# Two transformer blocks on one core: the second experts' order turned by sixteen, a hinted branch, and earlier weight splits in the first mixer

## The chip, the cores and the metric

The kernel runs on one core of a Trainium2 chip. The metric is the device time of one execution in microseconds (us), the median of several runs. TensorE (PE) does the matmuls, VectorE (DVE), ScalarE (ACT) and GpSimd (POOL) the elementwise work, and SyncE (SP) issues the loads of the weights.

## The reference, cut to what matters

Two different blocks follow each other on 256 tokens of width 1024, all in fp32. Each is a mixer (attention and a second branch, joined by an output projection) and a mixture of 32 experts in four groups of eight, of which a token uses two of one group. Cut to its core:

```python
# block 1: hybrid mixer, experts with 256 hidden columns, a shared expert
z = hp @ w_in                                   # c_q, c_kv, k_pe, gate_b, gate_c, x_in
q = rms_norm(c_q, q_norm) @ w_uq;  kv = rms_norm(c_kv, kv_norm) @ w_ukv
attn = causal_block_attention(...)              # 8 heads, 16 meta tokens ahead
conv = gate_b * sum(conv_w[k] * shifted(gate_c * x_in, k) for k in range(3))
h = h + rms_norm(concat(rms_norm(attn), rms_norm(conv)) @ w_out, post_mix_norm)
h = h + rms_norm(hier_moe(rms_norm(h, pre_ffn_norm)), post_ffn_norm)
# block 2: differential attention and retention, experts with 512 hidden columns
g_idx = argmax(softmax(t @ router_group + b));  e_idx = top_2(softmax(t @ router_expert + b)[g_idx])
routed = sum over the two experts of weight * (silu(t @ w_gate[e]) * (t @ w_up[e])) @ w_down[e]
```

The number of tokens that an expert gets depends on the data. With the inputs that the reference makes, every second-block expert has between 1 and 44 tokens but one: the thirtieth (index 29) has none. In the first block no expert has more than 32.

## The kernel before, in words

The program runs straight through: mixer 1, experts 1, mixer 2, experts 2, final norm. Weights stream through 26 slots of SBUF, each of 8 KB per partition. `plan()` is the fixed order of all weight chunks (1 MB each), and `Builder.load` issues them on SP's queue in that order. `ahead()` issues the next load whenever a slot has come free, so a load waits for the matmuls that last read its slot, and at most eight loads are under way.

**Experts 2** work in 16 units of two neighbouring experts, with room for 64 tokens per expert. A unit p has eight chunks of gate and up weights (`gu2`, even chunk numbers for the first expert of the unit, odd ones for the second) and four of down weights (`dn2`, likewise). The order is gu of unit p, then dn of unit p-1; only at the end dn of unit 14 comes ahead of gu of unit 15, with dn of unit 15 last. On PE a unit is `gate_up` (L1565, 64 matmuls), `down` of the unit before (L1645, 32 matmuls), a gather for every second unit (L1399), a transpose (L1592) and a scatter (L1671). Unit 15's down weights go through `quarters` (L1617). A load into a slot that held a chunk of these experts is conditional on the expert having tokens:

```python
e = 2 * key[1] + key[2] % 2          # some(), L276: expert of the chunk
return {"cond": self.loads_of[e] > 0}
```

The count is read into SP's registers. For an expert without tokens the transfer is left out, while its slot is still taken and the matmuls still run on what the slot held. An expert index 29 is the odd half of unit 14; index 13 would be the odd half of unit 6.

**Overflow.** `overflow()` (L1716) handles experts with more tokens than a unit holds (32 in block 1, 64 in block 2). It is a run-time branch, `tc.If` at L1738, built once for each block, after the fifth unit from the end is begun. With these inputs its body never runs.

**Mixer 1.** Many matmuls here multiply in three passes of a high and a low part. `prepare()` (L317) makes the parts of one half chunk: ACT copies 1024 columns to the high part (L329), and DVE (first half of a chunk) or POOL (second half) subtracts it for the low part (L330). `part()` hands the next prepared half to the matmuls (L354 to L356) and prepares another. `conv(i)` (L604) runs four such halves; `conv(0)` leaves its products in `u` (L622), later ones gate and filter (L631, L634). Ahead of `conv(0)` stands the norm of the compressed query and key, `cn` (L568 to L601, DVE, with a power on POOL at L366). `cn` is transposed into `cqT` (L657), which the query matmul (L675) reads. After the attention scores, `P` is normalised (L757 to L760, first half of the heads on DVE, second on POOL), transposed (L790), and `attend` (L805, L810) makes the output, whose projection is the last `w_out`, reading `ma`. At the end stands the first matmul of experts 1 (L1574).

Of the kernel before, what the change touches and what calls it, by code (L numbers as in the profile page):

```python
# [17 lines left out]
AF = mybir.ActivationFunctionType  # L18
OP = mybir.AluOpType
# [4 lines left out]
T = 256  # L24
# [51 lines left out]
def layout(i):  # L76
    f = {k: np.asarray(v) for k, v in i.items()}
    g = lambda n: f[n][0]
    o = {}
# [17 lines left out]
    def experts(n, wg, wu, wd):  # L97
        x, fw = 128 // CAP[n], wg.shape[2]
        fc = CH // (x * 512)
        if n == 2:  # L100
            gu = np.concatenate([wg, wu], 2).reshape(16, 2, 4, 2, 128, 1024).transpose(0, 2, 1, 4, 3, 5)
            dn = wd.reshape(16, 2, 4, 128, 2, 512).transpose(0, 4, 1, 3, 2, 5)
        else:
            gu = np.concatenate([wg, wu], 2).reshape(32 // x, x, 8, 128, 2 * fw).transpose(0, 2, 3, 1, 4)
            dn = wd.reshape(32 // x, x, fw // (128 * fc), fc, 128, 2, 512).transpose(0, 5, 2, 4, 3, 1, 6)
        o[f"gu{n}"], o[f"dn{n}"] = gu.reshape(-1, 8, 128, CH), dn.reshape(-1, 4, 128, CH)

    experts(1, g("w_gate"), g("w_up"), g("w_down"))
    experts(2, g("expert_w_gate_2"), g("expert_w_up_2"), g("expert_w_down_2"))
    last = g("expert_w_down_2")[30:].reshape(2, 4, 128, 4, 256).transpose(3, 2, 1, 0, 4)  # L110
    o["dn2"] = np.concatenate([o["dn2"][:-1], last.reshape(1, 4, 128, CH)], 0)
    w = kt(g("w_in_2"))
    nat = lambda a: w[:, :, a:a + 512].reshape(128, 2, CH).transpose(1, 0, 2)
    tr = lambda a: w[:, :, a:a + 512].reshape(128, 8, 2, 2, 128).transpose(2, 0, 3, 1, 4).reshape(2, 128, CH)
    o["wi2"] = np.stack([nat(1024), tr(0), tr(512), nat(2560), tr(1536), nat(2048)])
    o["wo2"] = kt(g("w_out_2")).reshape(128, 4, CH).transpose(1, 0, 2)
    o["wr"] = np.stack([np.concatenate([kt(g(a)), np.zeros((128, 8, 4), np.float32), kt(g(b))], 2).reshape(128, 320)
                        for a, b in (("w_group_router", "w_expert_router"),
                                     ("router_group_w_2", "router_expert_w_2"))])
    o["pmg"] = g("post_mix_norm")  # L120
    col = lambda v, n: v.reshape(n, 128).T
    row = lambda v: np.broadcast_to(v.reshape(1, -1), (128, v.size))
# [8 lines left out]
        "br2": np.concatenate([row(g("router_group_b_2")), pad, row(g("router_expert_b_2"))], 1),  # L131
# [59 lines left out]
class Builder:  # L191
# [120 lines left out]
    def bank(self):  # L312
        return self.ps.tile([128, 512], F32, name="bank")
# [126 lines left out]
    def mixer1(self):  # L440
# [86 lines left out]
                                   accum_out=ss[:, 3 * e + 1:3 * e + 2])  # L527
        V.tensor_tensor(ss[:, 0:3], ss[:, 0:3], ss[:, 3:6], op=OP.add)
        rx = self.rms(ss[:, 0:3], 3, D)
        ang = sub([128, 2, 3, 16])  # L530
        posf = sub([128, 3])
        nn = sub([128, 2, 3, 16])
# [20 lines left out]
        A.activation(sc, ang, AF.Sin)  # L553
        sin, cos = sc[:, 0], sc[:, 1]
        self.free(meta)
        self.prepare(2, V)
        nc.scalar.dma_start(cT[:, 1536:2048], self.a["c3"])
        rxx = sub([128, 258])

        def spread_rx():  # L560
            p = bank()
            self.spread(p[:, 0:NM], rx[:NM, 2:3], NM)
            for t in range(2):
                self.spread(p[:, NM + t * 128:NM + t * 128 + 128], rx[:, t:t + 1])
            A.activation(rxx, p[:, NM - 2:TA], AF.Square)

        ss2 = sub([128, 5])
        V.memset(ss2, 1.0)  # L568
# [23 lines left out]
        ru = sub([128, 256])  # L592
        rv = sub([128, 256])

        def rope(dst, src, cosb, sinb, n):
            u = ru[:, :32 * n].rearrange("p (a b c) -> p a b c", b=2, c=16)
            v = rv[:, :32 * n].rearrange("p (a b c) -> p a b c", b=2, c=16)
            V.tensor_tensor(u, src, cosb, op=OP.mult)
            V.tensor_tensor(v, src, sinb, op=OP.mult)
            V.tensor_tensor(dst[:, :, 0], u[:, :, 0], v[:, :, 1], op=OP.subtract)  # L600
            V.tensor_tensor(dst[:, :, 1], u[:, :, 1], v[:, :, 0], op=OP.add)  # L601
# [6 lines left out]
        def conv(i, done, then=(), between=()):  # L608
            for m in range(4):
                if m in then:  # L610
                    then[m]()
                w = self.part()
                c = w.rearrange("p s (k c) -> p s k c", k=8)
                p = bank()
                for k in range(8):
                    self.mm3(p[:, :258], (c[:, 0, k], c[:, 1, k]), (xh[k], xl[k]), k == 0, k == 7)
                if m in between:
                    between[m]()
                done(m, p[:, :258])
                self.free(w)  # L620

        conv(0, lambda m, p: V.tensor_tensor(u[:, m], p, rxx, op=OP.mult),  # L622
             between={0: spread_rx})

        vy = self.slot([128, 2048], "vy")
        v = vy[:, 0:1024].rearrange("p (t c) -> p t c", t=2)
# [14 lines left out]
        ckT = cT[:, 512:512 + TA]  # L641
        vm = cT[:, 1024:1536]
        pm = [(cT[:, 1536 + 256 * t:1664 + 256 * t], cT[:, 1664 + 256 * t:1792 + 256 * t]) for t in range(2)]
        pk = bank()
        PE.transpose(pk[:, 0:NM], cn[:NM, 2, 256:384], id_[:NM, :NM])
        for t in range(2):
# [5 lines left out]
        pq = bank()  # L652
        for j in range(2):
            for t in range(2):
                PE.transpose(pq[:, j * T + t * 128:j * T + t * 128 + 128], cn[:, t, j * 128:j * 128 + 128], id_)
        for j in range(2):
            V.tensor_scalar(cqT[:, j], pq[:, j * T:j * T + T], s["qn"][:, j:j + 1], None, op0=OP.mult)  # L657
# [98 lines left out]
        for e in range(2):  # L756
            for t in range(2):  # L757
                f = sm[:, t, 4 * e:4 * e + 4]
                V.reciprocal(f, f)
                (nc.gpsimd if e else V).tensor_tensor(P4(t, e), P4(t, e), f[:, :, None].to_broadcast(  # L760
                    [128, 4, 144 if t == 0 else TA]), op=OP.mult)
        self.free(gen)
        pT1 = self.slot([128, 2, 8, 128], "pT")
        at = cT[:, 0:1024].rearrange("p (t m q) -> p t m q", t=2, m=4)
# [54 lines left out]
                w_out(pc, mc, t, e, 2, w[0])  # L819
        for t in range(2):  # L820
            feat_tot(sq, t)
        self.prepare(2)
        self.phase(0, 6)
        turn_p(0, 0)
        turn_p(0, 1)
# [4 lines left out]
            w_out(pc, mc, 1, e, 3, w[1])  # L830
        turn_p(1, 1)
        self.free(*PP, *w, mc)
        rc = feat_rstd(rx[:, 0:2])
        turn_m(0)
        turn_m(1)
        mix = self.slot([128, 2, D], "mix")
        ma = self.slot([128, 2, 4, T], "ma", F32R)
        for t in range(2):
            for e in range(2):
                A.activation(mix[:, t, e * 512:e * 512 + 512], pc[t, e], AF.Copy, scale=rc[:, t:t + 1])  # L840
            attend(t)
        self.phase(0, 7)
        w = [self.part() for _ in range(4)]
        self.free(pT1, cT)
# [93 lines left out]
    def mixer2(self):  # L938
# [328 lines left out]
class MoE:  # L1267
# [215 lines left out]
    def run(self, after):  # L1483
# [236 lines left out]
        def overflow():  # L1720

            own = [b.slot([128, CH], "own") for _ in range(6)]
            b.quiet = True
            empty, b.empty = b.empty, collections.deque(b.held.pop(id(t))[0] for t in own if b.trace)
            ov = [b.slot([128, CH], "over") for _ in range(2)]
            keep = b.slot([128, 4, 512], "keep")
            xo = b.slot([128, 2, 8, 128], "xo")
            loads = [0]

            def load_over(name, *at):  # L1730
                t = ov[loads[0] % 2]
                loads[0] += 1
                nc.gpsimd.dma_start(t, a[name][at])
                return t

            over = nc.values_load(self.cnt[0:1, 0:1], min_val=0, max_val=T)
            held = 3 if n == 1 else 2
            with tc.If(over > C, preferred_fallthrough_block=False):  # L1738
                V.tensor_copy(keep[:, 3, :FW], hids[:, held, :FW])
                V.tensor_copy(keep[:, 2, 0:2], rs)  # L1740
                with tc.For_i(0, T // C - 1, 1):
                    V.tensor_scalar(rank, rank, float(-C), None, op0=OP.add)
                    slots(True)
# [77 lines left out]
```

## Time and profile before

| what | value |
|---|---|
| runs | 949.15, 949.41 and 949.89 us, median 949.41 |
| profiled execution | 944.73 us, of which the span from first to last instruction is 942.9 |
| PE busy | 853.1 us, 90% of the span |
| weight queue (q1) | 333.24 MB, its packets fill 86.5% of the span |
| mean granted TensorE clock | 0.946 of full speed |

Shares over the whole span hide the stages. Where the DMA share of a stretch stands at 1.01 the 16 DMA engines are full (about 420 GB/s), and where PE is busy for the whole of a stretch it waits for nothing. [...]

### The profile page before, as it was taken

Reading aid. Unit: us, or ns where it says so; the run is one execution under the profiler, and the core shown is the slowest. Engines: PE = TensorE matmul, PEld = TensorE weight load, DVE = VectorE, ACT = ScalarE, POOL = GpSimd, SP = SyncE. Lnnn points to the kernel's source line nnn. Section 1 sums busy time; section 2 is a strip of 40 time slices with the busy share of each in tenths; the row PEclk is TensorE's granted clock in tenths of the full one; section 3 lists DMA queues with packets and bytes.
Section 4 is the critical chain, followed back from the end, with each engine's and each line's share of the span. In section 5 each row is a group of like instructions: output and inputs, shape, how many; then the busy total and the mean of one; then the engine's idle time right before and its main releaser. Section 6 shows DMA issues by size and latency. Waiting matters only on the chain. (4 is left out here: it accounts for less than half of the span.)

```text
span 942.9 us, 12656 instructions
## 1 busy us (share of the span) xinstructions
PE 853.1 (90%) x4825; PEld 477.4 (51%) x4825; DVE 382.6 (41%) x787; ACT 228.3 (24%) x474; POOL 118.1 (13%) x83
## 2 busy tenths in 40 slices
PE   8899789999768777997999999999999998699995
PEld 6868565554313325897875444434343432334333
DVE  5766455244222248567552233233333312232233
ACT  5446332121101124653412112111111100111113
POOL 4321330000000038724310000000000000000002
PEclk8999989999878887997999999999999999899998
DMA  9927458999999999834688999999999999999981
GB/s 362 416 85 283 158 201 357 421 419 420 418 421 421 421 421 421 340 121 147 268 307 336 420 394 383 422 421 421 422 421 420 421 421 420 417 421 421 419 370 45
DMA packets 48187, 335.74 MB, mean 356 GB/s; under 512 B 5344, under 2 KB 5856, under 8 KB 8432
## 3 DMA queue, kind: packets, MB, share of 16 engines
q1 hardware_dynamic: 47072, 333.24, 86.5%
q10 hardware_dynamic: 1040, 1.54, 0.5%
q8 instruction: 43, 0.70, 0.3%
q14 instruction: 32, 0.26, 0.1%
HBM read 340.00 MB, written 1.05 MB: 362 GB/s over the span
## 5 line engine op out<-in xcount | busy, mean ns | idle before, releaser
L1565 PE MATMUL bank<-chunk,xe 128*64 128x512 f32 x1024 | 227.0, 599 | 8.6 <-issue 6.4
L1565 PEld LDWEIGHTS bank<-chunk,xe 128*64 128x64 f32 x1024 | 73.7, 138 | 152.7 <-issue 143.0
L1645 PE MATMUL bank<-chunk,hids 128*64 128x512 f32 x480 | 111.2, 594 | 4.5 <-DMA chunk<-in_dn_dram 4.5
L1574 PE MATMUL bank<-chunk,xe 128*32 128x512 f32 x512 | 66.1, 656 | 18.3 <-DMA chunk<-in_gu_dram 11.8
L330 POOL TENSOR_TENSOR w<-chunk,w 128x1024 fp32r<-128x1024 f32 x28 | 70.1, 2516 | 86.2 <-ACT w L329 73.4
L1660 DVE SCALAR_TENSOR_TENSOR ys<-bank,wc,ys 128x512 fp32r<-128x512 f32 x46 | 34.5, 750 | 101.8 <-ACT ys L1659 101.8
L1645 PEld LDWEIGHTS bank<-chunk,hids 128*64 128x64 f32 x480 | 35.4, 137 | 76.9 <-issue 66.0
L1580 DVE TENSOR_TENSOR hids<-bank,hids 128x512 f32<-128x512 f32 x12 | 8.3, 691 | 156.2 <-PE bank L1565 156.2
L1659 ACT ACTIVATE ys<-bank,wc 128x512 fp32r<-128x512 f32 x46 | 31.6, 687 | 142.6 <-PE bank L1645 107.7
L1243 POOL TENSOR_TENSOR out<-acc,rows 128x256 f32<-128x256 f32 x6 | 4.2, 730 | 437.7 <-DVE acc L1774 437.7
L329 ACT ACTIVATE w<-chunk 128x1024 fp32r<-128x1024 f32 x52 | 52.2, 1049 | 25.3 <-DVE w L330 11.5
L1678 DVE TENSOR_TENSOR acc<-acc,bank 128x512 f32<-128x512 f32 x84 | 52.1, 681 | 13.2 <-PE bank L1671 13.2
L1585 DVE SCALAR_TENSOR_TENSOR hids<-bank,misc,hids 128x256 f32<-128x256 f32 (+1 forms) x12 | 6.9, 573 | 114.2 <-ACT hids L1584 71.1
L1406 PEld LDWEIGHTS bank<-GS,h 128*128 128x128 f32 x384 | 46.6, 202 | 11.1 <-issue 5.4
L1671 PE MATMUL bank<-ys,GS 128*128 128x512 f32 x184 | 49.5, 408 | 1.4 <-ACT ys L1659 1.3
L1579 ACT ACTIVATE hids<-bank 128x512 f32<-128x512 f32 x12 | 7.2, 597 | 179.8 <-PE bank L1565 179.8
L1406 PE MATMUL bank<-GS,h 128*128 128x128 f32 x384 | 48.9, 288 | 1.6 <-DVE GS L1414 1.6
L1574 PEld LDWEIGHTS bank<-chunk,xe 128*32 128x32 f32 x512 | 15.8, 115 | 61.7 <-issue 59.7
L1656 PE MATMUL bank<-chunk,hids 128*32 128x512 f32 x256 | 36.1, 677 | 10.4 <-DMA chunk<-in_dn_dram 9.3
L330 DVE TENSOR_TENSOR w<-chunk,w 128x1024 fp32r<-128x1024 f32 x24 | 35.7, 1496 | 10.8 <-ACT w L329 10.8
L1584 ACT ACTIVATE hids<-bank,misc 128x256 f32<-128x256 f32 (+1 forms) x12 | 6.5, 545 | 136.3 <-PE bank L1574 88.4
L1006 PE MATMUL bank<-w,xT 128*128 128x512 f32 x144 | 37.7, 421 | 0.7 <-DVE xT L960 0.6
(409 smaller groups left out, 1260.3 us busy)
## 6 DMA issues: line engine op xcount, KB each, us to landing
chunk<-in_gu_dram SPq DMA_DIRECT2D x192, 1024.0 KB, 18.3
chunk<-in_dn_dram SPq DMA_DIRECT2D x95, 1024.0 KB, 19.8
chunk<-in_wi_dram SPq DMA_DIRECT2D x12, 1024.0 KB, 19.5
chunk<-in_wo_dram SPq DMA_DIRECT2D x8, 1024.0 KB, 15.4
chunk<-in_wc_dram SPq DMA_DIRECT2D x6, 1024.0 KB, 14.6
chunk<-in_sgu_dram SPq DMA_DIRECT2D x2, 1024.0 KB, 16.7
chunk<-in_wa_dram SPq DMA_DIRECT2D x4, 416.0 KB, 6.3
xt<-in_xt_dram SPq DMA_DIRECT2D x2, 512.0 KB, 4.3
```

Source lines behind the costliest of these rows:

```text
L329: self.nc.scalar.activation(w[:, 0], raw, AF.Copy)
L330: (eng or (self.nc.vector, self.nc.gpsimd)[e]).tensor_tensor(w[:, 1], raw, w[:, 0].bitcast(F32), op=OP.subtract)
L1006: PE.matmul(p[t], xT[x][:, 2 * i + k, t * 128:t * 128 + 128], w[:, s, k * 512:k * 512 + 512], start=i + x + s + k == 0, stop=i + x == 4 an ...
L1406: b.nc.tensor.matmul(self.pb[k // 4][:, k % 4 * 128:k % 4 * 128 + 128], b.h[:, t, k * 128:k * 128 + 128], G[:, t].bitcast(F32), start=t == ...
L1565: PE.matmul(g[i][e * C:e * C + C], xe[:, k + kk, e * C:e * C + C], cs[e][:, kk * 1024 + i * 512:kk * 1024 + i * 512 + 512], start=k + kk = ...
L1574: PE.matmul(g[i][e * C:e * C + C], xe[:, k, e * C:e * C + C], c[:, e, i * 512:i * 512 + 512], start=k == 0, stop=k == 7)
L1645: PE.matmul(y[e * C:e * C + C], hT[:, f * 128 + e * C:f * 128 + e * C + C], cs[e][:, f * 512:f * 512 + 512], start=f == 0, stop=f == 3)
L1656: PE.matmul(y[e * C:e * C + C], hT[:, o:o + C], c[:, f, e], start=q + f == 0, stop=fpc * q + f == FC - 1)
L1659: A.activation(ys[:, 0, i], y, AF.Copy, scale=wc)
L1660: V.scalar_tensor_tensor(ys[:, 1, i], y, wc, ys[:, 0, i].bitcast(F32), op0=OP.mult, op1=OP.subtract)
L1671: PE.matmul(ps[t], S[:, t * 128:t * 128 + 128], ys[:, i, e], start=i == 0, stop=i == 1)
L1678: V.tensor_tensor(o, b.h[:, t, sl] if new else o, p, op=OP.add)
```

## The change

Three separate things change.

1. The second block's experts are rolled by 16 in the layout: weights, router columns and bias. The unit that ran experts 16 and 17 now runs first. The kernel corrects the group numbers with two DVE instructions on 128x32 values in mixer 2. The expert without tokens moves from index 29 (unit 14) to index 13 (unit 6).
2. The overflow branch loses `preferred_fallthrough_block=False` and gets a hint, `LikelyTaken`, on all engines.
3. Mixer 1: `prepare(2, V)` ahead of the angles, `conv(0)` ahead of the `cn` block with a first `part(2)`, the `cqT` transposes ahead of those of the key with one of the two evacuations on ACT, `P`'s second half normalised on DVE, `prepare(2)` right behind it and another when `PP` is freed, and both `attend` ahead of the four `mix` evacuations on ACT.

```diff
+    turn = lambda w, axis: np.roll(w, -16, axis)
+    experts(2, *(turn(g(f"expert_w_{k}_2"), 0) for k in ("gate", "up", "down")))
...
+                                     (g("router_group_w_2"), turn(g("router_expert_w_2"), 1)))])
...
         rx = self.rms(ss[:, 0:3], 3, D)
+        self.prepare(2, V)
         ang = sub([128, 2, 3, 16])
...
-        self.prepare(2, V)
...
+        def conv(i, done, then=(), between=()):
...
+                w = self.part(2 if i + m == 0 else 1)
...
+        conv(0, lambda m, p: V.tensor_tensor(u[:, m], p, rxx, op=OP.mult),
+             between={0: spread_rx})
...
+        V.tensor_scalar(cqT[:, 0], pq[:, 0:T], s["qn"][:, 0:1], None, op0=OP.mult)
+        A.activation(cqT[:, 1], pq[:, T:2 * T], AF.Copy, scale=s["qn"][:, 1:2])
...
-                (nc.gpsimd if e else V).tensor_tensor(P4(t, e), P4(t, e), f[:, :, None].to_broadcast(
+                V.tensor_tensor(P4(t, e), P4(t, e), f[:, :, None].to_broadcast(
+        self.prepare(2)
         self.free(gen)
...
-        self.prepare(2)
         self.phase(0, 6)
...
         self.free(*PP, *w, mc)
+        self.prepare(2)
...
         for t in range(2):
+            attend(t)
+        for t in range(2):
             for e in range(2):
                 A.activation(mix[:, t, e * 512:e * 512 + 512], pc[t, e], AF.Copy, scale=rc[:, t:t + 1])
-            attend(t)
...
+        gid, over = self.k["gid"], misc[:, 1024:1056]
+        V.tensor_scalar(over, gid, 2.0, 4.0, op0=OP.is_ge, op1=OP.mult)
+        V.scalar_tensor_tensor(gid, gid, 2.0, over, op0=OP.add, op1=OP.subtract)
...
-            with tc.If(over > C, preferred_fallthrough_block=False):
+            tc.mark_branch_hint_location(f"over{n}", "LikelyTaken", engines=mybir.ALL_ENGINES)
+            with tc.If(over > C, label=f"over{n}"):
```

On PE, at the second block's overflow branch (L1738, in the changed file L1745), before:

```order
L1399 MATMUL bank<-GS,hh 128x256 x32
L1592 MATMUL bank<-const_72,hids 128x128 x4
L1671 MATMUL bank<-ys,GS 128x512 x8
L1736 TENSOR_LOAD misc
L1738 COMPARE_AND_BRANCH
L1738 UNCONDITIONAL_BRANCH
L1741 COMPARE_AND_BRANCH
L1741 UNCONDITIONAL_BRANCH x2
L1817 BRANCH_PREFETCH_HINT
L430 MATMUL bank<-const_72,misc 128x128 x4
```

and after:

```order
L1405 MATMUL bank<-GS,hh 128x256 x32
L1598 MATMUL bank<-const_72,hids 128x128 x4
L1677 MATMUL bank<-ys,GS 128x512 x8
L1742 TENSOR_LOAD misc
L1745 COMPARE_AND_BRANCH
L1748 COMPARE_AND_BRANCH
L1748 UNCONDITIONAL_BRANCH x2
L1824 BRANCH_PREFETCH_HINT
L431 MATMUL bank<-const_72,misc 128x128 x4
```

Before, a second, unconditional branch stood right behind the comparison and led over the body. After, the comparison itself leads to a block behind the body. The hint for it stands where the branch before it ended: at the program's start for the first block, at the end of the first block's overflow for the second.

On DVE, in mixer 1, from the end of the `cn` block (L599 to L601) to the first gated convolution (L631), before:

```order
L599 TENSOR_TENSOR gen_143<-gen_143 128x96
L600 TENSOR_TENSOR gen_143<-gen_143 128x3x16
L601 TENSOR_TENSOR gen_143<-gen_143 128x3x16
L622 TENSOR_TENSOR u<-bank,gen_143 128x258
L330 TENSOR_TENSOR w<-chunk,w 128x1024
L622 TENSOR_TENSOR u<-bank,gen_143 128x258 x2
L330 TENSOR_TENSOR w<-chunk,w 128x1024
L622 TENSOR_TENSOR u<-bank,gen_143 128x258
L631 TENSOR_TENSOR u<-bank,u 128x258
```

and after, from the split ahead of `conv(0)` into the `cn` block (in the changed file L597 to L619, then L574 to L577):

```order
L331 TENSOR_TENSOR w<-chunk,w 128x1024
L593 TENSOR_TENSOR u<-bank,gen_143 128x258 x2
L331 TENSOR_TENSOR w<-chunk,w 128x1024
L593 TENSOR_TENSOR u<-bank,gen_143 128x258 x2
L597 MEMSET gen_143 128x5
L599 MEMSET gen_143 128x32
L606 TENSOR_SCALAR gen_143<-gen_143 128x2
L607 TENSOR_SCALAR gen_143<-gen_143 128x3
L610 TENSOR_SCALAR gen_143<-bank,rs 128x32 x2
L611 TENSOR_SCALAR gen_143<-bank,rs 16x32
L613 TENSOR_TENSOR rs<-rs 128x2 x2
```

The splits and the four evacuations of `conv(0)` now stand ahead of the `cn` block, and the block stands between `conv(0)` and the gated convolutions.

On POOL, from the splits of the convolutions to the norm ahead of `attend` (L366, in the changed file L367), with the numbers of the tiles, before:

```order
L330 TENSOR_TENSOR w_772<-chunk_241,w_772 128x1024
L760 TENSOR_TENSOR P_845<-P_845,gen1_143 128x576
L760 TENSOR_TENSOR P_845<-P_845,gen1_143 128x1088
L330 TENSOR_TENSOR w_961<-chunk_243,w_961 128x1024
L330 TENSOR_TENSOR w_981<-chunk_245,w_981 128x1024
L366 TENSOR_TENSOR rs_1043<-ms_1041,mhalf_79 128x2
L330 TENSOR_TENSOR w_1105<-chunk_247,w_1105 128x1024
```

and after:

```order
L331 TENSOR_TENSOR w_717<-chunk_241,w_717 128x1024
L331 TENSOR_TENSOR w_807<-chunk_243,w_807 128x1024
L331 TENSOR_TENSOR w_966<-chunk_245,w_966 128x1024
L331 TENSOR_TENSOR w_1041<-chunk_247,w_1041 128x1024
L367 TENSOR_TENSOR rs_1051<-ms_1049,mhalf_79 128x2
```

The two normalisations have left POOL, and the split of the last chunk (247) stands ahead of the norm's power instead of behind it.

## Rows read from the trace of the kernel before

**Rows 1.** Stretches of the core; columns as the second line names them.
```profile
core 0: us, PE busy (x) PEld busy (x) DVE busy (x) ACT busy (x) POOL busy (x), PEclk, DMA share, GB/s
160.00:240.00 80.00, 73.93 (x524) 38.97 (x516) 29.72 (x64) 15.53 (x37) 0.00 (x0) 0.98 1.01 420
...
486.00:740.00 254.00, 251.62 (x1293) 113.84 (x1293) 79.27 (x180) 39.26 (x78) 0.56 (x1) 0.99 0.98 405
740.00:800.00 60.00, 54.50 (x254) 22.15 (x252) 16.06 (x32) 6.60 (x12) 0.00 (x0) 1.00 1.01 421
...
875.00:921.00 46.00, 45.95 (x216) 16.98 (x212) 11.48 (x21) 5.52 (x9) 0.00 (x0) 1.00 0.92 379
```

**Rows 2.** Waits of PE, 153 to 390: line, releaser, us, times, longest.
```profile
PE bank L1574 <- DMA chunk<-in_gu_dram: 11.8, 10, 2.1
```

**Rows 3.** Timeline of PE in experts 2: start, us, instructions, idle before.
```profile
600.92 13.96 PE L1565 MATMUL bank<-chunk,xe 128*64 128x512 f32 x64
...
624.13 13.96 PE L1565 MATMUL bank<-chunk,xe 128*64 128x512 f32 x64
...
651.17 11.38 PE L1565 MATMUL bank<-chunk,xe 128*64 128x512 f32 x52
...
724.63 13.96 PE L1565 MATMUL bank<-chunk,xe 128*64 128x512 f32 x64
...
820.11 10.20 PE L1565 MATMUL bank<-chunk,xe 128*64 128x512 f32 x36 [6.36 <-issue]
```

**Rows 4.** Chain that ended last, 800 to 943: start, us, what.
```profile
907.10 13.91 PE bank L1565 x64
...
923.25 3.67 PE bank L1617 x32
```

**Rows 5.** Timeline of SP: first issue, us to the last one's end, count.
```profile
612.76 15.39 SPq L274 DMA_DIRECT2D chunk<-in_gu_dram  x8
628.50 6.51 SPq L274 DMA_DIRECT2D chunk<-in_dn_dram  x4
...
866.26 8.22 SPq L274 DMA_DIRECT2D chunk<-in_dn_dram  x8
876.20 13.85 SPq L274 DMA_DIRECT2D chunk<-in_gu_dram  x8
```

**Rows 6.** Line L274, issues of 888 to 903.
```profile
DMA to landing us min/median/max: 17.3/18.7/20.2
```

**Rows 7.** DMA issues of 612 to 628: KB each, median us to landing.
```profile
chunk<-in_gu_dram SPq DMA_DIRECT2D x8, 1024.0 KB, 16.1
```

**Rows 8.** PE before the first block's branch, timeline 233 to 242.
```profile
240.62 1.94 PE L1574 MATMUL bank<-chunk,xe 128*32 128x512 f32 x8 [6.43 <-issue]
```

**Rows 9.** Waits of PE, 0 to 154.
```profile
PE bank L355 <- POOL w L330: 5.6, 2, 4.3
PE bank L356 <- DVE w L330: 2.8, 1, 2.8
PE bank L675 <- DVE cT L657: 2.1, 1, 2.1
...
PE bank L354 <- ACT w L329: 1.3, 1, 1.3
...
PE bank L355 <- DVE w L330: 0.9, 1, 0.9
```

**Rows 10.** Timeline of DVE, 28 to 60.
```profile
31.65 4.71 DVE L584 TENSOR_TENSOR rs<-rs 128x2 f32<-128x2 f32 x3 [0.82 <-POOL rs L366]
```

**Rows 11.** Timeline of POOL, 28 to 132.
```profile
31.58 7.10 POOL L330 TENSOR_TENSOR w<-chunk,w 128x1024 fp32r<-128x1024 f32 x3
...
111.36 0.69 POOL L366 TENSOR_TENSOR rs<-ms,mhalf 128x2 f32<-128x2 f32 x1 [4.79 <-DVE ms L371]
```

**Rows 12.** Stretches of mixer 1, columns as in group 1.
```profile
104.40:112.50 8.10, 6.90 (x33) 5.64 (x33) 2.19 (x8) 1.69 (x5) 2.87 (x2) 0.79 0.40 130
...
126.40:132.00 5.60, 5.60 (x16) 4.59 (x17) 0.91 (x2) 0.72 (x2) 1.90 (x2) 0.52 0.87 310
```

More of the change, by code (lines that the diff above doesn't have):

```diff
@@ L108, in layout @@
     experts(1, g("w_gate"), g("w_up"), g("w_down"))
-    experts(2, g("expert_w_gate_2"), g("expert_w_up_2"), g("expert_w_down_2"))
-    last = g("expert_w_down_2")[30:].reshape(2, 4, 128, 4, 256).transpose(3, 2, 1, 0, 4)
+    turn = lambda w, axis: np.roll(w, -16, axis)
+    experts(2, *(turn(g(f"expert_w_{k}_2"), 0) for k in ("gate", "up", "down")))
+    last = turn(g("expert_w_down_2"), 0)[30:].reshape(2, 4, 128, 4, 256).transpose(3, 2, 1, 0, 4)
     o["dn2"] = np.concatenate([o["dn2"][:-1], last.reshape(1, 4, 128, CH)], 0)
@@ L116, in layout @@
     o["wo2"] = kt(g("w_out_2")).reshape(128, 4, CH).transpose(1, 0, 2)
-    o["wr"] = np.stack([np.concatenate([kt(g(a)), np.zeros((128, 8, 4), np.float32), kt(g(b))], 2).reshape(128, 320)
-                        for a, b in (("w_group_router", "w_expert_router"),
-                                     ("router_group_w_2", "router_expert_w_2"))])
+    o["wr"] = np.stack([np.concatenate([kt(a), np.zeros((128, 8, 4), np.float32), kt(b)], 2).reshape(128, 320)
+                        for a, b in ((g("w_group_router"), g("w_expert_router")),
+                                     (g("router_group_w_2"), turn(g("router_expert_w_2"), 1)))])
     o["pmg"] = g("post_mix_norm")
@@ L130, in layout @@
         "br1": np.concatenate([row(g("b_group_router")), pad, row(g("b_expert_router"))], 1),
-        "br2": np.concatenate([row(g("router_group_b_2")), pad, row(g("router_expert_b_2"))], 1),
+        "br2": np.concatenate([row(g("router_group_b_2")), pad, row(turn(g("router_expert_b_2"), 0))], 1),
     }
@@ L565, in spread_rx, with rope @@
             A.activation(rxx, p[:, NM - 2:TA], AF.Square)
+        ru = sub([128, 256])
+        rv = sub([128, 256])
+        def rope(dst, src, cosb, sinb, n):
+            u = ru[:, :32 * n].rearrange("p (a b c) -> p a b c", b=2, c=16)
+            v = rv[:, :32 * n].rearrange("p (a b c) -> p a b c", b=2, c=16)
+            V.tensor_tensor(u, src, cosb, op=OP.mult)
+            V.tensor_tensor(v, src, sinb, op=OP.mult)
+            V.tensor_tensor(dst[:, :, 0], u[:, :, 0], v[:, :, 1], op=OP.subtract)
+            V.tensor_tensor(dst[:, :, 1], u[:, :, 1], v[:, :, 0], op=OP.add)
+        def conv(i, done, then=(), between=()):
+            for m in range(4):
+                if m in then:
+                    then[m]()
+                w = self.part(2 if i + m == 0 else 1)
+                c = w.rearrange("p s (k c) -> p s k c", k=8)
+                p = bank()
+                for k in range(8):
+                    self.mm3(p[:, :258], (c[:, 0, k], c[:, 1, k]), (xh[k], xl[k]), k == 0, k == 7)
+                if m in between:
+                    between[m]()
+                done(m, p[:, :258])
+                self.free(w)
+        conv(0, lambda m, p: V.tensor_tensor(u[:, m], p, rxx, op=OP.mult),
+             between={0: spread_rx})
         ss2 = sub([128, 5])
@@ L590, in mixer1 @@
             V.tensor_scalar(cn[:, t, 0:256], za[t][:, 0:256], r2[:, t:t + 1], None, op0=OP.mult)
[L592 to L601, printed above, removed]
         kr = sub([128, 3, 32])
@@ L606, in mixer1 @@
              sin[:, :, None, :].to_broadcast([128, 3, 2, 16]), 3)
[L608 to L623, printed above, removed]
         vy = self.slot([128, 2048], "vy")
@@ L643, in mixer1 @@
         pm = [(cT[:, 1536 + 256 * t:1664 + 256 * t], cT[:, 1664 + 256 * t:1792 + 256 * t]) for t in range(2)]
+        pq = bank()
+        for j in range(2):
+            for t in range(2):
+                PE.transpose(pq[:, j * T + t * 128:j * T + t * 128 + 128], cn[:, t, j * 128:j * 128 + 128], id_)
+        V.tensor_scalar(cqT[:, 0], pq[:, 0:T], s["qn"][:, 0:1], None, op0=OP.mult)
+        A.activation(cqT[:, 1], pq[:, T:2 * T], AF.Copy, scale=s["qn"][:, 1:2])
         pk = bank()
@@ L651, in mixer1 @@
                         None, op0=OP.mult)
[L652 to L657, printed above, removed]
         kT = [self.slot([96, 4, TA], "kT"), self.slot([96, 4, TA], "kT")]
@@ L838, in mixer1 @@
         for t in range(2):
+            attend(t)
+        for t in range(2):
             for e in range(2):
                 A.activation(mix[:, t, e * 512:e * 512 + 512], pc[t, e], AF.Copy, scale=rc[:, t:t + 1])
-            attend(t)
         self.phase(0, 7)
```

## The prediction

> **What bounds the kernel now.** I read the stretches of the core first, because the two limits change places. In experts 1 the DMA share stands at 1.01 while PE is not full [rows 1], and PE waits for gate and up chunks ten times [rows 2]: that stage goes at the pace of the weights, 420 GB/s, which is 2.50 us for a chunk of 1,048,576 bytes. In experts 2 both are nearly full from 486 to 740. From 740 to 800 PE is busy 54.50 of 60 us while the DMA is still full. From 875 to 921 PE is full again, and the DMA share falls to 0.92 because the last transfers are over before the stretch ends.
>
> The timeline of PE tells why [rows 3]. A pair of units takes 651.17 - 600.92 = 50.25 us, the one with a gather 651.17 - 624.13 = 27.04, so the other 23.21. Their mean is 25.1 us, while twelve chunks take 12 x 2.50 = 30.0. PE thus eats its lead over the weights, about 4.9 us a unit, and then waits. From 724.63 to 820.11 it needs 95.48 us for three units that are worth 50.25 + 27.04 = 77.29. Of the 18.19 lost, 6.36 is the stall at the branch [rows 3], and 11.83 is waiting for weights. Then comes the unit whose odd expert has no tokens. Its four gu chunks and two dn chunks are left out: the eight dn issues that follow go out in 8.22 us [rows 5] where eight chunks take 20.0 to transfer. From there the weights are ahead again and PE sets the end. Its gu of unit 15 begins at 907.10 and takes 13.91 [rows 4].
>
> **Part 1, the turned experts.** The bytes are the same; the gap in the stream moves from unit 14 to unit 6, whose loads are issued from 612.76 [rows 5]. Every chunk from there to unit 14 lands up to 6 x 2.50 = 15.0 us earlier. That covers the 11.83 us of waits, so they go, and PE would reach gu of unit 15 at about 907.10 - 11.83 = 895.3. But the weights at the end stand where they stood. The last gu issue goes out at 876.20 + 13.85 - 0.33 = 889.7 [rows 5], and its landing takes 17.3 to 20.2 us with a median of 18.7 [rows 6]. That group includes two short halves of 0.5 MB, which I put at its low end, so I take 19.5 for a full chunk: it lands at 909.2. The last pair of chunks feeds 16 of the 64 matmuls, 13.91 / 4 = 3.48 us. So gu of unit 15 ends at 912.7, where it ended at 907.10 + 13.91 = 921.0. The gain is 8.3 us (7.6 to 9.1 with the group's median and its maximum), not 11.8. What is late next is the weight stream itself. The work behind it, from 921.0 to the end at 942.9, is the same: unit 15's down weights are read from 923.25 on before, from 915 after. They come in four steps 2.5 us apart, about the pace at which they are used.
>
> The gain needs the DMA to stay full when chunks are skipped, since a slot that waits for PE can't be filled early. The eight gu issues of unit 6 take 15.39 us, and then four of dn 6.51 [rows 5]. These follow PE's release of slots and would not go out sooner. A median of 16.1 us from issue to landing [rows 7] is 6.4 chunks of work in the queue. Leaving out four, 10.0 us, leaves 6.1 us. So the queue just does not run dry before the next issues, and a loss of 0 to 4 us can't be excluded. Part 1 is thus worth 4 to 9 us, and I take 8.3. The bound of PE's own path, 11.8, would need a stream that ends sooner. The two new DVE instructions run on 32 columns. The nearest row has three on two columns in 4.71 us while POOL works beside them [rows 10, 11], so two cost between 0 (other work of mixer 2 hides them) and 3.1; I take 0, since PE's matmuls run beside them.
>
> **Part 2, the branch.** PE stands still for 6.36 us in experts 2 [rows 3] and 6.43 in experts 1 [rows 8]. The trace shows the length, not what the hint makes of it: bounds are 0 and the whole. In experts 1 the DMA stays full across the branch and the stage follows the weights, so its worth on the path is 0. In experts 2 PE waits for the stream at the end anyway: after part 1 it has 909.2 - 3.48 - 895.3 = 10.4 us that go into waits between the chunks of unit 15 and before it, so 6.36 more of lead is worth 0 too. I take 0 for both, with 0 to 1.
>
> [...]
>
> **Part 3, mixer 1.** What counts is when the first matmul of experts 1 runs, because it releases the slots for a stage that is bound by weights: a shift X there goes to the end in full. PE's waits for splits [rows 9] are 2.8 us (DVE, ahead of `conv(0)`), 4.3 of the 5.6 for POOL, and in the last projection 5.6 - 4.3 = 1.3 (POOL), 1.3 (ACT) and 0.9 (DVE), 3.5 in sum. Three changes:
> - The 2.8 us go, since the splits stand ahead of the `cn` block. But the block now runs behind `conv(0)`, and the gated convolutions and `cqT` come behind the block. PE already waits 2.1 us for `cqT` [rows 9]. The block includes 4.71 us for three instructions on two columns [rows 10], beside 7.10 us of POOL splits [rows 11]. If those shrink to nothing the block is hidden, and if they stay `cqT` is later by 4.7 us. I take 1.5 us later, because POOL's splits move ahead of the block and only one is left beside it; PE gains nothing from the 2.8.
> - The 4.3 us go, and so does the half clock behind them, 0.79 in the mean over 8.10 us [rows 12], 1.7 us. But POOL's last split (7.10 / 3 = 2.37 us [rows 11]) now stands ahead of the power (0.69 us [rows 11]) for which `attend` waits. With its load and ACT's copy ahead of it, I put the start of `attend` 1.5 us later than before (bounds: 3.5 earlier, if the load is there, to 3 later).
> - The 3.5 us in the last projection go. The half clock there (0.52 over 5.60 us [rows 12]) may go with them, up to 2.7 us, but a longer wait ahead of `attend` can bring it back: 0.
>
> The first term lies inside the second, which is measured at `attend`. So X = -1.5 + 3.5 = 2.0 us earlier, with bounds of -3 (`attend` 3 later, and the 3.5 turned into waits elsewhere) and +7 (3.5 + 3.5).
>
> The rows speak against part of it: DVE's three instructions on 128x2 take 1.6 us each while POOL splits [rows 10, 11]. [...]
>
> **Sum.** The profiled span of 942.9 becomes 942.9 - 8.3 - 2.0 = 932.6. The execution lies 1.8 above its span, so 934.4. It lies 4.7 below the median of the runs, 949.4; on that frame I predict 939.1 us.
>
> **Rivals.**
> - The stream paces the end as forecast, and mixer 1 gains all that its splits cost: X = 6, so 949.4 - 8.3 - 6 = 935.1. For it: the waits for splits are whole numbers in the trace [rows 9]. Against it: `cqT` is on the path already.
> - Mixer 1 becomes later: X = -3, so 949.4 - 8.3 + 3 = 944.1. For it: the lengths of DVE beside POOL [rows 10, 11] and the split ahead of the power. Against it: POOL loses its two normalisations.
> - Slower: at unit 6 the DMA runs dry. The issues there already wait for slots, so the six skipped transfers leave a hole that nothing fills, and the end of the stream moves by up to 15.0 us: 949.4 - 8.3 + 15.0 - 2.0 = 954.1. It decides from the point at which the queue holds less than the skipped 10.0 us; the rows put it at 16.1 [rows 7], 6.1 above. A partial hole of 8 us gives 947, no change.
> - The gap does not move, or the loads of unit 6 are made unconditionally: then only X is left, 947.4. Against it: the condition is the same code for both units.
>
> **Chances.** Forecast 0.56, mixer gains all 0.16, mixer later 0.13, hole at unit 6 0.10, gap not moved 0.05. The forecast's own range, with 4 us either way from X and the landing, is 935.5 to 943. With the first two rivals taken in, the range is 932.5 to 946. A measurement of this kernel tells about 0.2%, 1.9 us, from no change. Faster than 947.5 are the forecast and the first two rivals, and part of the last: 0.84. Same 0.06, slower 0.10.
>
> **What would show it.** After the change PE should have no waits for DMA from 740 to 875, and waits of some 2 us a pair for gu of unit 15 at the end. The DMA share should stay at 1.01 from unit 6 until the last issues land, and these should go out X earlier than before. If the share dips near 630 or 660, the hole is there. The stall at the branch may be there or gone without a shift of the end. In mixer 1 the wait for POOL at the transposes (4.3) should be gone, and a new one should stand ahead of `attend`. I am wrong if the end is bound by PE, or if the first matmul of experts 1 moves by over 7 us.

## The result, and the profile after

The changed kernel runs in 935.72 us (median; 934.38 to 937.83), the kernel before in 949.31 beside it. The ratio is 0.9858, with a 95% interval of 0.9839 to 0.9877: 13.6 us faster. The profiled execution took 934.38 with a span of 932.6, against 944.73 and 942.9.

Stretches of the core after, in experts 2, with the columns of [rows 1]:

```profile
740.00:800.00 60.00, 60.00 (x310) 27.72 (x306) 19.00 (x34) 10.15 (x19) 0.00 (x0) 1.00 1.01 421
800.00:820.00 20.00, 18.34 (x87) 7.41 (x88) 3.71 (x8) 1.28 (x2) 0.00 (x0) 1.00 1.02 418
820.00:875.00 55.00, 51.23 (x246) 22.37 (x244) 15.14 (x28) 5.92 (x11) 0.00 (x0) 1.00 1.01 421
875.00:913.00 38.00, 33.57 (x148) 13.09 (x146) 11.48 (x21) 5.53 (x9) 0.00 (x0) 1.00 1.01 419
```

From 740 to 800 PE, which was busy 54.50 us [rows 1], is now full. Its idle time lies behind 800: 1.66 us at the branch, and the rest behind 830, where it waits for weights. The DMA is now full up to 913. The chain that ended last, from 856 on, shows what that means (start, us, what):

```profile
856.88 10.36 PE bank L1571 x47
867.25 19.76 DMA chunk<-in_dn_dram
...
887.12 19.77 DMA chunk<-in_gu_dram
906.90 0.04 issue
906.94 3.66 PE bank L1571 x14
...
912.84 3.67 PE bank L1623 x32
```

Before, this part of the chain was PE alone, with gu of unit 15 whole, 64 matmuls from 907.10 [rows 4]. Now the chain goes from the last gu chunk's landing at 906.90 into the last 14 of these 64 matmuls, 3.66 us. The work behind it is the same. SP's issues around the skipped chunks and at the end, to be read against [rows 5], and below them the landing times that answer to [rows 6]:

```profile
610.90 15.15 SPq L275 DMA_DIRECT2D chunk<-in_gu_dram  x8
626.39 6.77 SPq L275 DMA_DIRECT2D chunk<-in_dn_dram  x4
...
869.74 17.72 SPq L275 DMA_DIRECT2D chunk<-in_gu_dram  x8
```

```profile
DMA to landing us min/median/max: 17.4/19.8/19.8
```

The issues of unit 6 go out at the same pace although four of the eight gu transfers are left out, and from 600 to 660 the DMA share is 1.01 after as before: the queue did not run dry. At the branch, the timeline of PE in experts 1 and 2 now reads:

```profile
234.39 7.07 PE L1580 MATMUL bank<-chunk,xe 128*32 128x512 f32 x64 [1.72 <-DVEq L1745]
...
801.82 13.95 PE L1571 MATMUL bank<-chunk,xe 128*64 128x512 f32 x64 [1.66 <-DVEq L1745]
```

PE's stall of 6.43 [rows 8] and 6.36 us [rows 3] has shrunk to 1.72 and 1.66. In mixer 1, PE's waits from 0 to 154 are other ones than in [rows 9]:

```profile
PE bank L676 <- DVE cT L649: 7.3, 1, 7.3
PE bank L807 <- DVE cT L377: 5.6, 1, 5.6
PE bank L792 <- ACT cT L379: 2.7, 1, 2.7
```

All waits for the halves that `prepare()` splits are gone. In their place PE waits 7.3 us for `cqT`, 2.7 at the transposes and 5.6 ahead of `attend`. The first matmul of experts 1 starts at 152.18, before at 153.69: 1.5 us earlier in these two executions.

### The profile page after: what moved, and what is told of

The parts are those of the page before. It is cut to its first block, busy times and chain, and to the rows that moved or that the text cites. A ratio compares the mean times of both kernels' runs of the same rounds, so it can differ in the third digit from the quotient of the medians.

```text
span 932.6 us, 12651 instructions
## 1 busy us (share of the span) xinstructions
PE 846.1 (91%) x4825; PEld 477.1 (51%) x4825; DVE 390.3 (42%) x790; ACT 228.3 (24%) x475; POOL 116.2 (12%) x81
## 3 DMA queue, kind: packets, MB, share of 16 engines
q1 hardware_dynamic: 47072, 333.24, 87.4%
## 4 chain that ended last, share of the span: by engine, by line
PE 45%; DMA 21%; DVE 4%; ACT 2%; issue 1%; POOL 1%; ACTq 0%; SPq 0%; POOLq 0%; DVEq 0%
PE bank L1571 19%; DMA chunk<-in_gu_dram 11%; DMA chunk<-in_dn_dram 11%; PE bank L1651 8%; PE bank L1677 2%; PE bank L1405 2%; PE bank L1412 2%; PE bank L355 2%; PE bank L357 2%; PE bank L356 2%; PE bank L1012 1%; PE bank L1598 1%; PE bank L1623 1%; ACT w L330 1%; DVE w L331 1%
## 5 line engine op out<-in xcount | busy, mean ns | idle before, releaser
L1651 PE MATMUL bank<-chunk,hids 128*64 128x512 f32 x480 | 108.7, 593 | 4.5 <-DMA chunk<-in_dn_dram 4.5
L331 POOL TENSOR_TENSOR w<-chunk,w 128x1024 fp32r<-128x1024 f32 x28 | 72.1, 2587 | 102.4 <-ACT w L330 80.9
L1580 PE MATMUL bank<-chunk,xe 128*32 128x512 f32 x512 | 63.8, 634 | 13.0 <-DMA chunk<-in_gu_dram 11.2
L1412 PEld LDWEIGHTS bank<-GS,h 128*128 128x128 f32 x384 | 47.7, 205 | 11.6 <-issue 6.8
L331 DVE TENSOR_TENSOR w<-chunk,w 128x1024 fp32r<-128x1024 f32 x24 | 37.5, 1569 | 13.7 <-ACT w L330 13.6
L1677 PEld LDWEIGHTS bank<-ys,GS 128*128 128x128 f32 x184 | 32.4, 188 | 11.1 <-ACT ys L1665 2.3
## 6 DMA issues: line engine op xcount, KB each, us to landing
chunk<-in_dn_dram SPq DMA_DIRECT2D x95, 1024.0 KB, 19.8
chunk<-in_wi_dram SPq DMA_DIRECT2D x12, 1024.0 KB, 19.5
```

The lines of the kernel that those rows point to most:

```text
L331: (eng or (self.nc.vector, self.nc.gpsimd)[e]).tensor_tensor(w[:, 1], raw, w[:, 0].bitcast(F32), op=OP.subtract)
L1412: b.nc.tensor.matmul(self.pb[k // 4][:, k % 4 * 128:k % 4 * 128 + 128], b.h[:, t, k * 128:k * 128 + 128], G[:, t].bitcast(F32), start=t == ...
L1580: PE.matmul(g[i][e * C:e * C + C], xe[:, k, e * C:e * C + C], c[:, e, i * 512:i * 512 + 512], start=k == 0, stop=k == 7)
L1651: PE.matmul(y[e * C:e * C + C], hT[:, f * 128 + e * C:f * 128 + e * C + C], cs[e][:, f * 512:f * 512 + 512], start=f == 0, stop=f == 3)
L1677: PE.matmul(ps[t], S[:, t * 128:t * 128 + 128], ys[:, i, e], start=i == 0, stop=i == 1)
```

## The experiments

All ratios are to the kernel before, run on the same chip between the runs.

**One part at a time.** The three parts of the diff were put into the kernel before alone, and the changed kernel was run without the hint:

```diff
# roll_only:  only   turn = lambda w, axis: np.roll(w, -16, axis)  with its uses, and the gid lines
# hint_only:  only   tc.mark_branch_hint_location(...), tc.If(over > C, label=...)
# mixer_only: only   the edits in mixer1
# roll_mixer: the changed kernel with  tc.If(over > C, preferred_fallthrough_block=False)
```

> The kernel before with the turned experts alone. Theory (the weight stream paces the end once the gap in it lies at unit 6): gu of unit 15 ends 3.5 us after its last chunk, about 8 us earlier than before; 8 us off the time, ratio about 0.9915, PE waits for weights inside gu of unit 15, and the stall of some 6.4 us at the branch stays without cost. Rival (PE's own path sets the end): 11.8 us off, ratio 0.9876, no waits at the end. Rival (the stall, still there, is on the path): 8 - 4.7 = 3.3 us off.

Measured 942.0 us, ratio 0.9921 (0.9906 to 0.9937): 7.5 us off (7.75 by the medians). The theory holds: both rivals, 11.8 and 3.3 us, lie outside the interval. The last gu chunk is waited for until 914.86, and the last 14 matmuls of unit 15's gu come behind it, as the chain of this kernel shows:

```profile
895.07 19.75 DMA chunk<-in_gu_dram
914.86 3.66 PE bank L1569 x14
```

The stall at the branch is still there (PE stands still for 6.55 us ahead of 814.16) and costs nothing.

> The kernel before with the hinted branch alone. Theory: the stall of PE shrinks from 6.4 to about 1.7 us in both expert stages, but both follow the weights there; in experts 2 the chunks of units 12 and 13 land when they did, so PE waits for them in place of the stall. 0 to 1 us off, ratio 0.999 to 1.000. Rival (the stall is on the path): 4.7 us off for one stage, 9.4 for both, ratio 0.995 or 0.990.

Measured 948.56 against 949.75, ratio 0.9993 (0.9984 to 1.0003): no difference that can be told. PE's waits from 738 to 880 show where the gain at the branch went:

```profile
PE bank L1645 <- DMA chunk<-in_dn_dram: 7.3, 6, 1.3
PE bank L1565 <- DMA chunk<-in_gu_dram: 4.5, 4, 1.3
PE bank L1565 <- DVEq L1739: 1.7, 1, 1.7
```

The same view of the kernel before, 738 to 875:

```profile
PE bank L1565 <- issue: 6.4, 1, 6.4
PE bank L1645 <- DMA chunk<-in_dn_dram: 4.5, 5, 1.3
PE bank L1565 <- DMA chunk<-in_gu_dram: 2.3, 2, 1.3
```

The branch costs 4.7 us less, and the waits for weights grow from 6.8 to 11.8, by 5.0. What the hint gives, the stream takes.

> The kernel before with the edits of mixer 1 alone. Theory: the first matmul of experts 1 runs 1.5 us earlier (as in the changed kernel), and that shift passes in full through the stage that weights pace to the end: 1.5 to 2.3 us off, ratio about 0.998. Rival (a later stage takes the shift up): 0 us off.

Measured 945.04, ratio 0.9954 (0.994 to 0.9968): 4.4 us off, more than the theory's 1.5 to 2.3. It passes to the end, but its size was wrong. The starts in the traces show why. The table gives, for one profiled execution each, the first matmul of `attend`, the first of experts 1, PE's granted clock between these two, the first matmul of experts 2, the end, and the time from experts 2 to the end. The last four rows are kernels of the experiments further down, which share one of the two mixers:

| kernel | mixer 1 | attend | experts 1 | clock between | experts 2 | end | experts 2 to end |
|---|---|---|---|---|---|---|---|
| before | old | 112.51 | 153.69 | 0.92 | 499.89 | 942.95 | 443.1 |
| hint_only | old | 115.60 | 157.36 | 0.92 | 503.46 | 946.99 | 443.5 |
| roll_only | old | 114.76 | 159.49 | 0.81 | 505.74 | 940.48 | 434.7 |
| mixer_only | new | 113.91 | 154.31 | 0.83 | 502.03 | 945.56 | 443.5 |
| roll_mixer | new | 113.81 | 154.18 | 0.83 | 501.89 | 937.48 | 435.6 |
| after | new | 113.66 | 152.18 | 0.88 | 498.28 | 932.56 | 434.3 |
| late_two_before | old | 112.64 | 157.36 | 0.81 | 504.34 | 947.25 | 442.9 |
| late_two | new | 114.61 | 154.95 | 0.83 | 502.65 | 933.05 | 430.4 |
| roll8 | new | 113.64 | 152.20 | 0.88 | 498.38 | 932.46 | 434.1 |
| roll24 | new | 113.83 | 154.14 | 0.83 | 501.84 | 951.44 | 449.6 |

With the old mixer the start of experts 1 lies anywhere from 153.69 to 159.49, and the profiled execution of before is the earliest of them. With the new mixer it lies from 152.18 to 154.95. The means (157.0 and 153.7) are 3.3 us apart, where the two executions compared above are 1.5 apart. Much of the spread goes with the granted clock at the end of mixer 1: with the old mixer the stretch from `attend` to experts 1 takes 41.2 and 41.8 us where the clock was 0.92, and 44.7 twice where it was 0.81; with the new one 38.5 to 38.6 at 0.88 and 40.3 to 40.4 at 0.83. Of the 5.8 us by which roll_only starts later than before, 3.5 lie in this stretch and the other 2.3 ahead of `attend`. PE's waits in mixer 1 do not explain the 3.5: they are like those of [rows 9] (4.9, 4.4 and 2.1 us for the first three). Why the clock differs between executions of the same code stays open.

> The changed kernel without the hint, the branch as before. Theory: the stall of 6.4 us is back on PE in both stages, but the stream sets the end: the same as the changed kernel within 1 us, ratio to the kernel before about 0.989. Rival (the changed kernel owes part of its gain to the hint): 4.7 us slower than the changed kernel, ratio about 0.994.

Measured 938.3, ratio 0.9884 (0.9866 to 0.9901). This is 2.5 us above the changed kernel by the ratios, with overlapping intervals: neither the theory's 1 us nor the rival's 4.7 is shown by the times. In the trace the stretch from the first matmul of experts 2 to the end is 435.6 us with the old branch and 434.3 with the hint, so in these two executions not over 1.3 us of it is the hint's.

**Does the stream set the end?** Two late loads were left out, in the changed kernel and in the one before:

```diff
         some = self.some(key) if kept else {}
+        if kept and key in (("dn2", 13, 2), ("dn2", 13, 3)):
+            return
```

> The changed kernel without the loads of the last two chunks of dn of unit 13 (their matmuls run on what the slots held). Theory (the stream sets the end after the change): two chunks of 2.5 us less ahead of gu of unit 15, so the end comes 4 to 5 us earlier than in the changed kernel, about 931, ratio to the kernel before 0.981. Rival (PE's own path sets the end): 0 us against the changed kernel, about 0.986.

> The kernel before without the same two loads. Theory (with the gap in the stream at unit 14, PE sets the end): the two chunks come behind the gap, where PE waits for nothing: 0 us off, ratio 1.000 within 0.001. Rival (the stream sets the end there too): 4 to 5 us off, ratio 0.995.

The changed kernel gave 932.37, ratio 0.9823 (0.9796 to 0.985), 3.5 us below the 935.89 of roll8, which ran beside it, and 3.4 below the changed kernel; the stretch from experts 2 to the end fell from 434.3 to 430.4. The kernel before gave 949.44, ratio 1.0005 (0.9988 to 1.0021), no change. So the stream sets the end after the change, and before it these two loads were worth nothing. The gain is below the 5.0 us of the two transfers because PE is next. The chain without the two loads:

```profile
857.17 20.09 DMA chunk<-in_dn_dram
877.30 7.08 PE bank L1653 x30
...
886.83 7.02 PE bank L1653 x32
...
897.10 13.91 PE bank L1573 x64
```

Behind 877.30 it is PE that sets the pace, with all 64 matmuls of unit 15's gu in one piece again. From that landing on, PE's path is some 4 us shorter than the stream's was. Ahead of it PE still waits for weights, so how early PE alone could end is not shown.

**Where the gap may lie.** The roll by other amounts, with the group numbers set to match:

```diff
# roll8                                              # roll24
+    turn = lambda w, axis: np.roll(w, -8, axis)     np.roll(w, -24, axis)
+        ... op0=OP.is_ge with 3.0, then gid + 1.0   is_ge with 1.0, then gid + 3.0
```

> The changed kernel with the experts rolled by 8 in place of 16: the expert without tokens runs in unit 10. Theory: the place does not matter as long as it lies ahead of the waits and far enough behind the stretch in which loads wait for slots: the same as the changed kernel within 1 us, ratio 0.986. Rival (PE's lead must be built before 740): PE waits about 1.5 to 4 us ahead of unit 10 and ends that much later.

Measured 935.89, ratio 0.9877 (0.9848 to 0.9905), with a span of 932.5 against 932.6: the same as the changed kernel within the intervals. Unit 10 is as good as unit 6.

> The changed kernel with the experts rolled by 24: the expert without tokens runs in unit 2, whose loads are issued from about 480 to 520, where loads wait for slots and the queue is short. Theory of the prediction's slower rival, tried where its condition holds: the skipped transfers leave a hole of 8 to 12 us in the stream that nothing fills (one odd chunk of the unit is loaded in any case, 2.5 more), and the end comes 8 to 15 us later than in the changed kernel, about 944 to 950, ratio about 0.995 to 1.000. Rival (the queue covers the hole as at unit 6): the same as the changed kernel, 0.986.

Measured 953.25, ratio 1.0039 (1.002 to 1.0057): slower than the kernel before, and 17.4 us above roll8. The stretches of this kernel and then of the changed one, same columns:

```profile
500.00:520.00 20.00, 20.00 (x109) 10.12 (x109) 3.60 (x17) 6.26 (x14) 0.00 (x0) 0.92 0.70 262
520.00:540.00 20.00, 20.00 (x103) 7.78 (x103) 4.30 (x12) 3.00 (x7) 0.00 (x0) 1.00 0.81 325
540.00:560.00 20.00, 20.00 (x112) 10.20 (x110) 5.83 (x12) 2.32 (x6) 0.00 (x0) 1.00 0.88 345
560.00:600.00 40.00, 40.00 (x216) 18.76 (x213) 15.16 (x27) 7.84 (x13) 0.00 (x0) 1.00 0.90 368
```

```profile
500.00:520.00 20.00, 20.00 (x118) 10.05 (x116) 4.44 (x15) 5.58 (x15) 0.00 (x0) 1.00 0.84 335
520.00:540.00 20.00, 20.00 (x100) 7.55 (x97) 3.76 (x7) 2.07 (x3) 0.00 (x0) 1.00 1.01 421
540.00:560.00 20.00, 20.00 (x108) 9.37 (x108) 5.51 (x12) 2.32 (x6) 0.00 (x0) 1.00 0.98 398
560.00:600.00 40.00, 40.00 (x222) 20.26 (x220) 17.01 (x31) 9.32 (x17) 0.00 (x0) 1.00 0.97 400
```

Against a full share of 1.01, the idle time of the DMA is 6.2 + 4.0 + 2.6 + 4.4 = 17.2 us here and 3.4 + 0 + 0.6 + 1.6 = 5.6 there: a hole of 11.6 us (13.6 by the bytes of the last column, at 421 GB/s). With one chunk more on the queue (334.29 MB for 333.24, 2.5 us) that is 14.1 to 16.1. In the table above, roll24 takes 449.6 us from experts 2 to the end where the changed kernel takes 434.3, so hole and chunk account for the 15.3 between them; another 3.6 of the difference of the two executions lie ahead of experts 2. The queue was short there already in the kernel before, whose loads of 488 to 512 landed sooner than the 16.1 us of [rows 7]:

```profile
chunk<-in_gu_dram SPq DMA_DIRECT2D x8, 1024.0 KB, 9.8
```

PE is full in all these rows. The hole is paid later, in waits for weights: 14.8 us here from 486 to the end, where the same view of the changed kernel has 6.6.

```profile
PE bank L1651 <- DMA chunk<-in_dn_dram: 9.0, 10, 1.4
PE bank L1571 <- DMA chunk<-in_gu_dram: 5.8, 5, 1.3
```

**Which edit of mixer 1 counts.** Three edits of the changed kernel, and two together:

```diff
# cn_first: conv(0, ...) moved back behind the rope of kr
# norm_on_pool
-                V.tensor_tensor(P4(t, e), P4(t, e), ...
+                (nc.gpsimd if e else V).tensor_tensor(P4(t, e), P4(t, e), ...
# attend_first
         self.free(*PP, *w, mc)
-        self.prepare(2)
         rc = feat_rstd(rx[:, 0:2])
         turn_m(0)
         turn_m(1)
+        self.prepare(2)
# both: cn_first and attend_first
```

> The changed kernel with conv(0) put back behind the cn block, its other edits kept. Theory: PE's wait of 7.3 us for cqT comes from the block's new place on DVE; with the block ahead the wait is 2 to 3 us again and one of up to 2.8 us for DVE's split may come back ahead of it: 2 to 3 us faster than the changed kernel. Rival (the place of the block is what shortens mixer 1): 2 us or more slower.

Measured 936.2, ratio 0.9867 (0.9843 to 0.9891): the same as the changed kernel, between the two theories. PE's waits in mixer 1:

```profile
PE bank L357 <- DVE w L331: 2.7, 1, 2.7
...
PE bank L676 <- DVE cT L649: 1.9, 1, 1.9
...
PE bank L357 <- POOL w L331: 1.0, 1, 1.0
```

The 7.3 us for `cqT` have turned back into 2.7, 1.9 and 1.0 for splits and `cqT`, 5.6 in sum, and the first wait of the program grew in this execution, 2.5 for 1.3. `attend` starts at 113.91, where in the changed kernel it starts at 113.66: moving the block gains nothing either way.

> The changed kernel with the second half of P normalised on POOL as before. Theory: the old wait of some 4 us at the transposes comes back, because POOL's split stands behind the two normalisations: 1 to 3 us slower than the changed kernel. Rival (the edit does nothing, since DVE's longer queue takes as much): within 1 us.

Measured 933.99, ratio 0.9848 (0.9825 to 0.9872): not slower, so the theory falls. PE waits 1.2 us for POOL's normalisation in place of 2.7 for ACT's copy, and for no split there. The move of the normalisation brought nothing; in this execution `attend` starts at 111.28, 2.4 us earlier than in the changed kernel, so it may have cost something, but by the times that is not shown.

> The changed kernel with the last prepare(2) of mixer 1 moved behind the norm ahead of attend, so that POOL's power and DVE's small instruction no longer stand behind splits. Theory: PE's wait of 5.6 us ahead of attend falls to 2 us or less, the first matmul of experts 1 is some 3.5 us earlier, and all of it reaches the end: 3 to 4 us faster than the changed kernel. Rival (the splits are then late for the last projection): 0 us, with waits for splits there.

Measured 931.94, ratio 0.9818 (0.9792 to 0.9845): 3.8 us below the changed kernel's median, and 17 below the kernel before. The intervals overlap by a little, but `both` below gives the same time. The timelines of DVE and POOL in the changed kernel, and then of POOL in this one, with PE's wait:

```profile
108.53 1.23 DVE L331 TENSOR_TENSOR w<-chunk,w 128x1024 fp32r<-128x1024 f32 x1 [1.88 <-ACT w L330]
109.67 2.29 DVE L782 TENSOR_TENSOR chunk<-rs 128x2 f32<-128x2 f32 x1
...
109.52 2.43 POOL L331 TENSOR_TENSOR w<-chunk,w 128x1024 fp32r<-128x1024 f32 x1 [9.18 <-ACT w L330]
112.52 0.70 POOL L367 TENSOR_TENSOR rs<-ms,mhalf 128x2 f32<-128x2 f32 x1 [0.56 <-DVE ms L372]
```

```profile
107.90 0.70 POOL L367 TENSOR_TENSOR rs<-ms,mhalf 128x2 f32<-128x2 f32 x1 [7.40 <-DVE ms L372]
109.52 3.01 POOL L331 TENSOR_TENSOR w<-chunk,w 128x1024 fp32r<-128x1024 f32 x1 [0.93 <-ACT w L330]
```

```profile
PE bank L807 <- DVE cT L377: 1.0, 1, 1.0
```

In the changed kernel POOL is done with its split before the power is due: it stands idle for 0.56 us and waits for DVE. What makes the power late is DVE, which waits 1.88 us for ACT's copy, splits for 1.23, and then takes 2.29 for an instruction on two columns (L782), which lasts until POOL's split ends. Here L782 runs at 106.67 and takes 0.15. The power now runs ahead of the split, the wait ahead of `attend` falls from 5.6 to 1.0, `attend` starts 4.6 us earlier and experts 1 at 149.51, 2.7 earlier; the clock between the two was 0.83, where it was 0.88. With `both`, this is the fastest version.

> The changed kernel with both of the edits named for cn_first and attend_first. Theory: the two waits are apart, so the gains add up: 5 to 7 us faster than the changed kernel, about 929 to 931. Rival (half clock or another wait takes one of them): 3 us.

Measured 932.35, ratio 0.9818 (0.9793 to 0.9842), as attend_first alone: with cn_first worth nothing, there is nothing to add.

## Why the prediction was right, point by point

The forecast was 939.1 us, the time is 935.72, at the edge of the forecast's own range (935.5 to 943). On the profiled execution's own frame it was 934.4, and that is what was measured, 934.38. To that digit it is luck: in the two traces the stretch from experts 2 to the end fell by 8.8 us where 8.3 were forecast, and the start of experts 1 moved by 1.5 where 2.0 were. By the time alone the first rival (mixer 1 gains all that its splits cost, 935.1) fits as well. Its mechanism does not, since new waits took the place of those for splits; its 6 us lie just outside the 3.0 to 5.7 that mixer 1 alone gave, as the forecast's 2.0 do.

- **Part 1, the turned experts: right.** Forecast 8.3 us; alone it gave 7.5 (6.0 to 8.9 by its interval). The last chunk's landing was put 19.5 us behind its issue and took 19.8. The chain goes through that landing into the last 14 of unit 15's 64 gu matmuls, and PE's waits for weights moved from 740 to 820 behind 830. The 11.83 us that these waits were to cost PE are right too, though the view of waits counts only 6.8: PE went from 724.63 to 820.11, 95.48 us, through what took it 722.79 to 801.82 after, 79.03, and 4.70 of the difference is the branch, which leaves 11.75. The two new DVE instructions, put at 0, cost nothing that shows: from the start of experts 1 to that of experts 2 it is 347.7 us both in mixer_only, which lacks them, and in roll_mixer, which has them. My expectation that PE would have none from 740 to 875 was too clean: after 830 it waits for weights again, since it had caught up already.
- **The slower rival: right in mechanism, wrong place for this change.** At unit 6 the queue held, as the 6 us to spare that [rows 5, 7] gave had it. At unit 2 it did not, and the gain of the changed kernel was lost, with 3.7 us more.
- **Part 2, the hint: right.** 0 taken, -0.3 to 1.5 us measured. The stall did shrink by 4.7 us of 6.4, and PE's waits for weights took these up, as forecast. PE stands still for 1.72 us in experts 1 and 1.66 in experts 2 at the hinted jump, for 6.43 [rows 8] and 6.36 [rows 3] before. Both parts of the edit, the hint and the place of the body, came together, and which did it was not tried.
- **Part 3, mixer 1: the direction right, the size too small.** The term "X = 2.0 us earlier" measured 4.4 (3.0 to 5.7). In the two profiled executions it was 1.5. The mis-sized step was to read X off one execution of the kernel before and to add the frame of 4.7 us unchanged. That execution has the earliest start of experts 1 of the four with the old mixer, 3.3 us ahead of their mean, so most of the frame seems to be the old mixer's later starts; after the change the frame is 1.3. The half clock in the last projection (0.52 over 5.60 us [rows 12]), put at 0, belongs to this step: the old mixer's last stretch took 3.5 us more in the two executions at 0.81. Inside X, the wait for `cqT` grew as foreseen (forecast 1.5 us later; 57.02 against 55.90 for the matmul behind it, 1.1). The new wait ahead of `attend` appeared where it was forecast, 1.2 us later than before (113.66 against 112.51; 1.5 taken), but not by the forecast's way. POOL's split stands ahead of the power, yet the power did not wait for it; it waited for DVE, whose own split and whose L782 beside POOL's split were late. That the size came out is luck. The 3.5 us of waits in the last projection went; the stretch from `attend` to experts 1 got 2.7 us shorter, at a clock of 0.88 for 0.92.
- **DVE beside POOL.** The three instructions on two columns that took 4.71 us [rows 10] take 0.30 after, with no split beside them, and DVE's splits that took 1.21 take 2.65 and 2.74 beside POOL's. In attend_first an instruction of the same shape, L782, takes 0.15 us with POOL idle, and in the changed kernel 2.29 beside POOL's split. Such lengths spoke for the second rival, a later mixer 1. It fell, since mixer 1 became earlier: alone it gave 4.4 us (3.0 to 5.7).

## What to carry to other kernels

When two limits are nearly equal, ask of each gap in the stream where it is spent: in this kernel a transfer left out where PE set the pace was worth nothing, and left out where the queue was short it was a hole that was paid at the end. Read the queue's depth (time from issue to landing over the time of one transfer) before moving such a gap: it was 6.4 transfers at unit 6 and 3.9 at unit 2. A small instruction on the critical path belongs ahead of bulk work, on its own engine and on the one beside it: one `prepare(2)` put behind the norm took 3.8 us off, more than either of the other two edits of mixer 1 that were tried. And one trace is one execution: before a shift of 2 us is read off it, see how far the same stretch moves between executions, and at what granted clock.

## What the runs showed of the hardware that was not expected

A run-time branch with the jumped body behind a direct jump and a hint stalled PE for 1.7 us, where a short block with a second jump stalled it for 6.4; this was so in both stages. The starts of experts 1 spread by 5.8 us between single executions of kernels with the same mixer 1. In the stretch that ends there, executions of the same code ran at a granted clock of 0.92 or 0.81 with the old mixer and took 41 or 45 us. So one trace is not enough to size an edit of 2 us there.
